# The last group of experts: the overflow loop between its two pairs, the second pair's weights loaded ahead of it, rows returned by index in halves, own sum first

## The chip, the cores and the metric

The kernel runs on one core of a Trainium2 chip. The metric is the device time of one execution in microseconds (us). TensorE is PE in the rows, VectorE DVE, ScalarE ACT, GpSimd POOL and SyncE SP; SP issues most of the DMA transfers, POOL those that go by an index.

## The reference, cut to what matters

512 tokens of 1024 features go through two blocks of a transformer. The first ends with a hierarchical mixture of experts: each token picks one of 4 groups and, in it, 2 of 8 experts with hidden width 256. The second begins with a norm and a sparse attention layer (DSA) and goes on with more layers. All tensors are fp32. What the change touches is the end of the first block and the start of the second:

```
for g in range(N_GROUPS):                       # 4 groups of 8 experts
    a = einsum('td,edf->tef', t, w_gate[sl]);  u = einsum('td,edf->tef', t, w_up[sl])
    hid = silu(a) * u * combine[:, g, :, None]  # combine: 0 but for a token's 2 experts
    y = y + einsum('tef,efd->td', hid, w_down[sl])
x = x + gt2[:, None, :] * ffn
...
return rms_norm(x, g_final)                     # end of block 1
h = rmsnorm(x, g_attn[0]); proj = h @ w_in      # start of block 2 (DSA)
```

## The kernel before, in words

The activations lie transposed in `xT`: eight blocks `k` of 128 features x 512 tokens. `moe` runs the 32 experts in eight units of four; a unit is two pairs, and each expert takes 64 slots. A ninth unit (`None` in `units`) takes tokens that found no slot. For a pair `q` of unit `u`, written (u,q) here, `up` multiplies the gathered tokens with the gate and up weights of both experts (32 matmuls, `s<-wm,xg`) and makes `hid` on ACT and DVE; `down` transposes `hid` (`o`), copies it (`ht`) and multiplies with the down weights (16 matmuls, `t<-wm,ht`). `load_expert` brings an expert in as four gate/up tiles and two down tiles of 512 KB each, issued by SP; all have the tag `wm`, of which there are 12 buffers, so the 12 tiles of one pair fill the tag and a tile's load waits until the tile 12 places before it has been read.

Units 0 to 6 and the ninth write their result rows by an index to a table in DRAM (`ydr`, issued by POOL). Unit 7 keeps its rows on the core as a rounded part and a rest (`yh`, `yl`); `scatter` adds them to `xT` by matmul with a 0/1 matrix `dt` (`mm<-dt,yh`, `mm<-dt,yl`, four for each `k`), and DVE adds the result to `xT[:, k]`. `combine` fetches the table's rows back, two per token: eight gathers of 128 rows x 1024 by index on POOL (`yg<-ydr,yrowi`), weighted on ACT and added on DVE. `add_combined` transposes that sum on PE (`mm<-ident,yg`, 32 of them) and adds it to `xT` on DVE.

Before the change the order in `moe` is: (7,0) up and down, `combine`, (7,1) up and down, `add_combined`, the overflow loop, `scatter`. The overflow loop (`For_i(0, n)`) handles overflow beyond the ninth unit; with these inputs `n` is 0 and its body is not run. All engines go through its branches all the same. `norm_dsa` loads two weights of the DSA layer (`a_w_idx`, `a_w_in`) into `wm` buffers, and ACT and POOL split them (`wf`); it is called when unit 7 starts, so these loads stand on SP's queue ahead of unit 7's weights.

`scatter(prev, range(KD), done)` calls `done(k)` once `xT[:, k]` is complete: it makes the norm's squares (`sq`: two on ACT, their sums on DVE and on POOL) and the split of the normed block (`xh` on ACT, `xl` on DVE), and PE multiplies these with `wf` (48 matmuls `s<-xh,wf`, `s<-xl,wf`). After the last block PE sums the squares (`o<-ones,sq`) and goes on with the projections of DSA (`mm<-xh,wh` and the like), whose weights arrive as `wr` and are split into `wh` (ACT) and `wl` (DVE or POOL). The masks `ms` and `cm` of DSA are made on POOL in the same stretch. Instructions of one engine run in the order of their queue, which the tile scheduler fixes when the kernel is built.

Of the kernel before, what the change touches and what calls it, by code (L numbers as in the profile page):

```python
# [9 lines left out]
F32 = mybir.dt.float32  # L10
# [8 lines left out]
KD = 8  # L19
# [16 lines left out]
class Kern:  # L36
# [804 lines left out]
    def route(self, rn, pl):  # L841
# [173 lines left out]
        st.yrow = ph.tile([128, 4, 2], I32, name="yrowi")  # L1015
        nc.vector.tensor_copy(st.yrow, yrow)
# [30 lines left out]
    def down(self, st, q, ws, hid):  # L1047
# [28 lines left out]
        if yh:  # L1076
            st.ys.append((yh, yl))

# [94 lines left out]
    def combine(self):  # L1173

        nc, r = self.nc, self.rt
        zs = []
        for t in range(4):
            y = []
            for j in range(2):
                w = self.ph.tile([128, 2, 512], F32, tag="wm", name="yg", bufs=12).rearrange("p h n -> p (h n)")  # L1180
                nc.gpsimd.indirect_dma_start(out=w, out_offset=None, in_=self.ydr[:, :],
                                             in_offset=bass.IndirectOffsetOnAxis(ap=r.yrow[:, t, j:j + 1], axis=0))
                y.append(w)
            nc.scalar.activation(out=y[0], in_=y[0], func=AF.Copy, scale=r.wts[:, t, 0:1])
            nc.vector.scalar_tensor_tensor(out=y[1], in0=y[1], scalar=r.wts[:, t, 1:2], in1=y[0], op0=OP.mult, op1=OP.add)
            zs.append(y[1])
        return zs

    def add_combined(self, zs):
        nc = self.nc  # L1190
        for k in range(KD):
            pt = self.bank("mm")
            for t in range(4):
                nc.tensor.transpose(pt[:, 128 * t:128 * t + 128], zs[t][:, 128 * k:128 * k + 128], self.ident)
            nc.vector.scalar_tensor_tensor(out=self.xT[:, k], in0=pt, scalar=self.mod[:, 40 + k:41 + k], in1=self.xT[:, k], op0=OP.mult, op1=OP.add)

    def moe(self, done=None):
# [23 lines left out]
        for j, u in enumerate(units):  # L1221
            m = len(st.es)
            if st.row is None:
                self.untranspose(st)
            nxt = None
            if j + 1 < len(units):
                u = units[j + 1]
                nxt = self.over_unit(r.oslot, r.ids, Y_OVER) if u is None else self.base_unit(u)
            for q in range(m):
                x = self.up(st, q, lambda e: self.early.pop(e) if isinstance(e, int) and e in self.early else self.load_expert(e))  # L1230
                if nxt is not None:
                    self.gather(nxt, range(4 // m * q, 4 // m * (q + 1)))
                self.down(st, q, *x)
                if nxt is None and q == 0:
                    zs = self.combine()
            prev, st = st, nxt
            if done and j == len(units) - 2:
                self.norm_dsa()
        self.add_combined(zs)
# [4 lines left out]
        nc.vector.tensor_copy(ids2, r.ids[:, 0:16])  # L1244
        with self.tc.For_i(0, n, 1):
            nc.vector.tensor_scalar(os2, os2, -128.0, None, op0=OP.add)
            t = ph.tile([1, 16], I32, name="idst")
            nc.vector.tensor_copy(t[:, 0:14], ids2[:, 2:16])
            nc.vector.tensor_copy(ids2[:, 0:14], t[:, 0:14])
            st = self.over_unit(os2, ids2)  # L1250
            self.gather(st, range(4))
            self.untranspose(st)
            self.down(st, 0, *self.up(st, 0, self.load_expert))
            self.scatter(st, range(KD))
        self.scatter(prev, range(KD), done)
# [743 lines left out]
```

## Time and profile before

| | us |
|---|---|
| median of 3 runs | 1982.56 |
| lowest and highest run | 1979.72, 1983.92 |
| profiled execution | 1980.94 |
| its span in the trace | 1979.2 |
| its mean granted TensorE clock | 0.981 of full speed |
| PE busy, of the span | 1894.1 (96%) |
| DVE, ACT, POOL busy | 951.0 (48%), 743.9 (38%), 292.5 (15%) |

The trace is of one execution, the profiled one; its times count from the start of the span. The change touches some 120 us of it, from about 690 to 810. PE's 96% is busy time of pipelined matmuls, and it averages stages with different limits: where weights stream in at full rate, DMA sets the pace, and PE is merely seldom idle for long. So the stretch is read by what each engine waits for in it.

### The profile page before, as it was taken

What the parts mean: (1) busy time and instruction counts of PE and PEld (TensorE: products, weight loads), DVE (VectorE), ACT (ScalarE), POOL (GpSimd) and SP (SyncE); (2) the same over time, 40 slices, a digit from 0 to 9 for tenths busy, and PEclk for the clock granted to TensorE, in tenths of its full rate; (3) what the DMA queues carried; (4) which work ended last, traced back from release to release, by engine and by line L of the source; (5) the groups of instructions that cost most, each with busy time, mean ns of one, the idle gap of its engine ahead of it and who ended that gap; (6) DMA issues with size and microseconds to landing.
All of it is one profiled execution on the core that took longest, in us unless ns stands there. A gap on an engine that the chain in (4) does not pass through costs nothing.

```text
span 1979.2 us, 26110 instructions
## 1 busy us (share of the span) xinstructions
PE 1894.1 (96%) x9778; PEld 1453.0 (73%) x9778; DVE 951.0 (48%) x2024; ACT 743.9 (38%) x1374; POOL 292.5 (15%) x353
## 2 busy tenths in 40 slices
PE   9999999999988868889999999999999999999998
PEld 6777778885544325568888888887889988888886
DVE  5677764461000025766644444464366553444343
ACT  3555552232211224556332322341455444223233
POOL 2212220000011024575000000000143300000001
PEclk9999999999999988879999999999999999999999
DMA  7523648347999994011223222225410122323221
GB/s 263 189 95 124 206 146 271 111 162 296 365 367 359 358 353 160 33 33 43 96 93 99 96 96 96 96 97 180 139 44 23 43 97 85 96 96 96 96 97 63
DMA packets 91328, 289.85 MB, mean 146 GB/s; under 512 B 13694, under 2 KB 14718, under 8 KB 91200
## 3 DMA queue, kind: packets, MB, share of 16 engines
q1 hardware_dynamic: 87520, 280.35, 40.5%
q0 software_dynamic: 3392, 7.29, 1.0%
q8 instruction: 78, 1.28, 0.3%
q10 hardware_dynamic: 288, 0.52, 0.1%
q14 instruction: 50, 0.41, 0.1%
HBM read 274.02 MB, written 18.35 MB: 148 GB/s over the span
## 4 chain that ended last, share of the span: by engine, by line
PE 55%; DVE 2%; POOL 1%; issue 1%; ACT 1%; DVEq 0%; POOLq 0%; ACTq 0%
PE mm L50 38%; PE s L50 7%; PE t L50 5%; PE o L50 4%; PE t L245 1%; DVE sc L1438 1%; POOL qal L65 0%; DVE m L1437 0%; DVE p L231 0%; POOL p L236 0%; POOL wl L65 0%; POOL ql L65 0%; PE t L1595 0%; DVE sc L1420 0%; POOL sc L1423 0%
## 5 line engine op out<-in xcount | busy, mean ns | idle before, releaser
L61 ACT CAST wh<-wr 128x1024 fp32r<-128x1024 f32 (+1 forms) x222 | 230.9, 1041 | 577.6 <-PE mm L50 312.6
L67 DVE TENSOR_TENSOR wl<-wr,wh 128x1024 fp32r<-128x1024 f32 (+1 forms) x216 | 263.9, 1222 | 315.2 <-ACT wh L61 311.9
L50 PE MATMUL mm<-xh,wh 128*128 128x512 f32 (+1 forms) x640 | 252.6, 395 | 0.0
L50 PE MATMUL mm<-xl,wh 128*128 128x512 f32 (+1 forms) x640 | 250.1, 391 | 0.0
L50 PE MATMUL mm<-xh,wl 128*128 128x512 f32 (+1 forms) x640 | 250.0, 391 | 0.0
L50 PE MATMUL s<-wm,xg 128*64 128x512 f32 x528 | 139.2, 603 | 5.6 <-DMA wm<-in_w_gu 5.4
L50 PEld LDWEIGHTS mm<-xh,wh 128*128 128x128 f32 (+1 forms) x640 | 119.9, 187 | 28.4 <-issue 2.2
L50 PEld LDWEIGHTS mm<-xh,wl 128*128 128x128 f32 (+1 forms) x640 | 119.9, 187 | 26.0
L50 PEld LDWEIGHTS mm<-xl,wh 128*128 128x128 f32 (+1 forms) x640 | 119.8, 187 | 25.0 <-issue 0.5
L234 ACT ACTIVATE p<-p,mx 128x128 f32<-128x128 f32 (+3 forms) x160 | 89.7, 561 | 91.9 <-DVE mx L233 87.4
L50 PEld LDWEIGHTS s<-wm,xg 128*64 128x64 f32 x528 | 42.0, 138 | 85.9 <-issue 73.5
L1044 DVE TENSOR_TENSOR hid<-hid,s 128x256 f32<-128x256 f32 x17 | 7.2, 421 | 199.5 <-ACT hid L1043 199.5
L50 PE MATMUL mm<-hidh,wh 128*128 128x512 f32 x256 | 99.6, 389 | 0.0
L50 PE MATMUL mm<-hidl,wh 128*128 128x512 f32 x256 | 99.6, 389 | 0.0
L50 PE MATMUL mm<-hidh,wl 128*128 128x512 f32 x256 | 99.6, 389 | 0.0
L236 POOL TENSOR_SCALAR p<-p,mx 128x128 f32<-128x128 f32 (+3 forms) x96 | 60.1, 629 | 153.0 <-DVE mx L235 97.5
L50 PE MATMUL mm<-hh,wh 128*128 128x512 f32 x192 | 77.9, 407 | 1.5 <-ACT hh L61 1.5
L231 DVE CUSTOM_DVE_ANT_0 p<-s,ms 128x256 f32<-128x256 f32 (+3 forms) x128 | 61.3, 487 | 35.6 <-PE s L50 30.2
L50 PE MATMUL mm<-hl,wh 128*128 128x512 f32 x192 | 76.4, 398 | 0.8 <-DVE hl L67 0.8
L50 PE MATMUL mm<-hh,wl 128*128 128x512 f32 x192 | 75.9, 395 | 0.0
L245 PE MATMUL t<-ident,p 128*128 128x128 f32 x400 | 69.8, 281 | 6.0 <-POOL p L236 5.8
L61 ACT CAST hidh<-r 128x512 fp32r<-128x512 f32 x64 | 39.7, 621 | 85.0 <-DVE r L1259 85.0
(607 smaller groups left out, 3984.3 us busy)
## 6 DMA issues: line engine op xcount, KB each, us to landing
wm<-in_w_gu SPq DMA_DIRECT2D x132, 512.0 KB
wm<-in_w_dn SPq DMA_DIRECT2D x66, 512.0 KB
wr<-in_w_up SPq DMA_DIRECT2D x64, 512.0 KB
wr<-in_w_down SPq DMA_DIRECT2D x64, 512.0 KB
wr<-in_w_ada SPq DMA_DIRECT2D x48, 512.0 KB
wr<-in_w_in SPq DMA_DIRECT2D x22, 512.0 KB
ydr<-zero SPq DMA_DIRECT2D x32, 256.0 KB
wr<-in_cmp_w SPq DMA_DIRECT2D x16, 512.0 KB
```

Of the source, the lines that this page charges most:

```text
L50: return self.nc.tensor.matmul(ps, lhsT=l, rhs=r, start=start, stop=stop)
L61: nc.scalar.copy(hi, src)
L67: return nc.vector.tensor_tensor(out=lo, in0=src, in1=fv(hi), op=OP.subtract)
L231: nc.vector.tensor_tensor_reduce(out=p[:, :n], in0=s[:, :n], in1=master[:, c0:c0 + n], scale=1.0, scalar=-3.0e38, op0=OP.add, op1=OP.max, ...
L234: nc.scalar.activation(out=p[:, :n], in_=p[:, :n], func=AF.Exp, bias=mx[:, 1:2], accum_out=mx[:, 2:3])
L236: nc.gpsimd.tensor_scalar(p[:, :n], p[:, :n], mx[:, 3:4], 1.0 if gate is None else gate, op0=OP.mult, op1=OP.mult)
L245: nc.tensor.transpose(ps[:, b], p[:, b], self.ident)
L1044: nc.vector.tensor_tensor(out=hid, in0=hid, in1=ps[:, 256:512], op=OP.mult)
L1438: nc.vector.match_replace(out=sc[:, :n], in_to_replace=m8, in_values=sc[:, :n], imm_value=-3.0e38)
```

## The change

1. In `moe` the order becomes: (7,0) up and down; both experts of (7,1) loaded; the overflow loop; (7,1) up and down; `combine`; `norm_dsa`; `scatter`; `add_combined`. The ninth unit and units 1 to 6 are as before.
2. `combine` fetches rows in halves of 512 columns: 16 gathers of 128 x 512 instead of 8 of 128 x 1024, from the same table seen as rows twice as many, with two index tiles (`yrowi0`, `yrowi1`). They go into buffers of another pool and no longer into `wm`. A copy of one column of a weight tile of (7,1) on POOL (`mark`) stands ahead of the gathers.
3. The unit's own rows are added first (`scatter`, without `done`), the fetched ones last, and `add_combined` calls `done(k)`.
4. The body of the loop uses narrow buffers of its own (`narrow_pair`); `no_sync_barrier` is called ahead of the loop.
5. `norm_dsa` moves behind the loop, and with it the loads of `a_w_idx`, `a_w_in` and of nine small vectors (gains of norms).

The core of the diff:

```diff
-        st.yrow = ph.tile([128, 4, 2], I32, name="yrowi")
-        nc.vector.tensor_copy(st.yrow, yrow)
+        st.yrow = [ph.tile([128, 4, 2], I32, name=f"yrowi{h}") for h in range(2)]
+        for h in range(2):
+            nc.vector.tensor_scalar(st.yrow[h], yrow, 2.0, float(h), op0=OP.mult, op1=OP.add)
...
-    def combine(self):
+    def combine(self, behind):
         nc, r = self.nc, self.rt
+        ydr = self.ydr.rearrange("n (f d) -> (n f) d", f=2)
+        mark = self.small.tile([128, 1], F32, tag="mark", name="mark", bufs=1)
+        last = nc.gpsimd.tensor_copy(mark, behind)
         zs = []
-        for t in range(4):
-            y = []
-            for j in range(2):
-                w = self.ph.tile([128, 2, 512], F32, tag="wm", name="yg", bufs=12).rearrange("p h n -> p (h n)")
-                nc.gpsimd.indirect_dma_start(out=w, out_offset=None, in_=self.ydr[:, :],
-                                             in_offset=bass.IndirectOffsetOnAxis(ap=r.yrow[:, t, j:j + 1], axis=0))
-                y.append(w)
...
+        for h in range(2):
+            z = []
+            for t in range(4):
+                y = []
+                for j in range(2):
+                    y.append(self.X("yg"))
+                    with self.tc.issue_after(last.ins):
+                        nc.gpsimd.indirect_dma_start(out=y[j], out_offset=None, in_=ydr,
+                                                     in_offset=bass.IndirectOffsetOnAxis(ap=r.yrow[h][:, t, j:j + 1], axis=0))
+                nc.scalar.activation(out=y[0], in_=y[0], func=AF.Copy, scale=r.wts[:, t, 0:1])
+                nc.vector.scalar_tensor_tensor(out=y[1], in0=y[1], scalar=r.wts[:, t, 1:2], in1=y[0], op0=OP.mult, op1=OP.add)
...
+        self.down(st, 0, *self.up(st, 0, load))
+        ws = [self.load_expert(e) for e in st.es[1]]
+        behind = ws[1][0][0][:, 0:1]
         n = nc.values_load(r.ids[0:1, 16:17], min_val=0, max_val=7)
...
+        self.tc.no_sync_barrier()
         with self.tc.For_i(0, n, 1):
...
-        self.scatter(prev, range(KD), done)
+        self.down(st, 1, *self.up(st, 1, lambda e: ws.pop(0)))
+        zs = self.combine(behind)
+        if done:
+            self.norm_dsa()
+        self.scatter(st, range(KD))
+        self.add_combined(zs, done)
```

**The queue of SP around the loop.** Before: the two DSA weights, then four experts' weights (unit 7), then the loop's branches; the last row is that in front of which the engine goes on behind a loop that is not run.

```order
L1285 DMA wm<-in_a_w_idx 128x576
L1285 DMA wm<-in_a_w_in 128x1024
L1025 DMA wm<-in_w_gu 128x1024 x4
L1029 DMA wm<-in_w_dn 128x1024 x2
L1025 DMA wm<-in_w_gu 128x1024 x4
L1029 DMA wm<-in_w_dn 128x1024 x2
L1025 DMA wm<-in_w_gu 128x1024 x4
L1029 DMA wm<-in_w_dn 128x1024 x2
L1025 DMA wm<-in_w_gu 128x1024 x4
L1029 DMA wm<-in_w_dn 128x1024 x2
L1245 COMPARE_AND_BRANCH
```

After: the same unit's last two weight tiles, the loop's branches with what SP waits for on the way past the body, and what follows the loop. Semaphores `DMAHW0` to `DMAHW7` count the transfers that SP issues.

```order
L1031 DMA wm_6225<-in_w_dn 128x1024 [waits DMAHW6_49,PE_49]
L1031 DMA wm_6227<-in_w_dn 128x1024 [waits DMAHW7_49,PE_49]
L1293 COMPARE_AND_BRANCH
L1293 UNCONDITIONAL_BRANCH [waits SP_sequencer_49,DMAHW0_49,DMAHW1_49,DMAHW2_49,DMAHW3_49,DMAHW4_49,DMAHW5_49,DMAHW6_49,DMAHW7_49]
...
L352 DMA v_g_mlp1_13828<-in_g_mlp1 128x8 [waits DMAHW4_49]
L1338 DMA wm_6601<-in_a_w_idx 128x576 [waits DMAHW5_49,PE_49]
L1338 DMA wm_6612<-in_a_w_in 128x1024 [waits DMAHW6_49,PE_49,Pool_49]
...
L1317 DMA ms_7524<-in_rel_bias_2 128x512 [waits DMAHW6_49,PE_49]
L87 DMA wr_6866<-in_a_w_in 128x1024 [waits DMASW4_49,DMASW3_49,DMASW5_49,DMASW2_49,DMASW6_49,DMASW1_49,DMASW7_49,DMASW0_49,DMAHW7_49,DVE_49,Pool_49]
```

The DSA weights moved from ahead of unit 7's weights to behind the loop. The way past the loop's body carries a wait on all eight counters of SP's transfers; in the program the values waited for are those of every transfer issued up to there (752 on each counter in the kernel after, 768 or 784 in the one before), and the other engines wait for the same counters before they go on. The first projection weight `wr` now waits for all gathers (`DMASW`), for DVE and for POOL; in the kernel before it has no wait.

**The queue of POOL behind the last table write.** Before (`wf`: split of the DSA weights; `yg`: the gathers):

```order
L1066 DMA ydr<-y,wrow 4352x512
L65 TENSOR_TENSOR wf<-wm,wf 128x512 x2
L1181 DMA yg<-ydr,yrowi 128x1024 x8
L1240 TENSOR_LOAD ids
L1245 COMPARE_AND_BRANCH
L1245 UNCONDITIONAL_BRANCH x2
```

After, from the loop's end to the first split of a projection weight:

```order
L1219 COPY mark<-wm 128x1
L1228 DMA yg<-ydr,yrowi_4406 128x512 x8
L1228 DMA yg<-ydr,yrowi_4407 128x512 x8
L1318 AFFINE_SELECT ms<-ms 128x512 x2
L65 TENSOR_TENSOR wf<-wm,wf 128x288
...
L65 TENSOR_TENSOR wf<-wm,wf 128x512
L1318 AFFINE_SELECT ms<-ms 128x512
L1442 MEMSET cm 128x512
L1443 AFFINE_SELECT cm<-cm 128x512
L179 TENSOR_TENSOR sq<-sq 128x512 x5
L65 TENSOR_TENSOR wl<-wr,wh 128x1024 x3
```

The gathers and the four `wf` moved behind the loop and stand ahead of the squares; the first `wl` moved from between the second and the third `sq` to behind the last.

**The queue of DVE behind the loop.** Before, from unit 7's last `yl` on, it holds 8 additions to `xT` (L1121), 8 `xl` and 7 `sq` up to the sums. After, it begins so:

```order
L1046 TENSOR_TENSOR hid<-hid,s 128x256
L68 SCALAR_TENSOR_TENSOR yl<-t,cws,yh 128x512
L1161 SCALAR_TENSOR_TENSOR xT<-mm,mod,xT 128x512
L68 SCALAR_TENSOR_TENSOR yl<-t,cws,yh 128x512
L1161 SCALAR_TENSOR_TENSOR xT<-mm,mod,xT 128x512 x4
L1231 SCALAR_TENSOR_TENSOR yg<-yg,wts 128x512
L1161 SCALAR_TENSOR_TENSOR xT<-mm,mod,xT 128x512
L1231 SCALAR_TENSOR_TENSOR yg<-yg,wts 128x512
```

It goes on with six more `yg`, eight additions of fetched rows (L1242), 7 `sq` and 8 `xl`: from the first `yl` to the last `xl` 41 instructions of 512 columns. Eight `yg` of 512 (four of 1024 before), eight additions and the `yl` moved behind the loop.

## Rows read from the trace of the kernel before

**Rows 1.** Page, part 2: GB/s moved in each of 40 slices.

```profile
GB/s 263 189 95 124 206 146 271 111 162 296 365 367 359 358 353 160 33 33 43 96 93 99 96 96 96 96 97 180 139 44 23 43 97 85 96 96 96 96 97 63
```

**Rows 2.** Windows: stretch, length, busy time of each engine, PEclk, DMA share, GB/s.

```profile
708.00:712.00 4.00, 2.24 (x6) 0.68 (x8) 0.00 (x0) 0.00 (x0) 1.23 (x2) 0.75 1.02 410
...
748.00:756.00 8.00, 4.69 (x20) 1.26 (x18) 1.92 (x3) 2.13 (x4) 0.00 (x0) 1.00 0.02 6
```

**Rows 3.** Timeline of PE: start, length, instruction, count, [idle before, releaser].

```profile
709.76 8.78 PE L50 MATMUL s<-wm,xg 128*64 128x512 f32 x30 [4.03 <-DMA wm<-in_w_gu]
722.33 0.44 PE L1051 MATMUL o<-ident,hid 128*128 128x128 f32 x2 [3.79 <-DVE hid L1044]
723.28 5.35 PE L50 MATMUL t<-wm,ht 128*64 128x512 f32 x16 [0.52 <-issue]
...
741.52 7.08 PE L50 MATMUL s<-wm,xg 128*64 128x512 f32 x30
...
750.43 3.65 PE L50 MATMUL t<-wm,ht 128*64 128x512 f32 x16 [0.46 <-ACT ht L1053]
757.16 0.50 PE L50 MATMUL mm<-dt,yh 128*128 128x512 f32 x1 [3.07 <-DVEq L1245]
```

**Rows 4.** Timeline of SP's queue of DMA issues, same columns.

```profile
691.45 0.33 SPq L1285 DMA_DIRECT2D wm<-in_a_w_idx  x1
...
742.19 0.85 SPq L1029 DMA_DIRECT2D wm<-in_w_dn  x2
```

**Rows 5.** Timeline of DVE, same columns.

```profile
741.07 1.41 DVE L1195 SCALAR_TENSOR_TENSOR xT<-mm,mod,xT 128x512 f32<-128x512 f32 x2 [0.19 <-PE mm L1194]
...
753.23 0.75 DVE L68 SCALAR_TENSOR_TENSOR yl<-t,cws,yh 128x512 fp32r<-128x512 f32 x1 [3.75 <-ACT yh L63]
754.88 0.75 DVE L68 SCALAR_TENSOR_TENSOR yl<-t,cws,yh 128x512 fp32r<-128x512 f32 x1 [0.91 <-ACT yh L63]
...
782.67 1.78 DVE L179 TENSOR_TENSOR sq<-sq 128x512 f32<-128x512 f32 x1
```

**Rows 6.** Groups on DVE, 757 to 787: shapes, count, busy us, mean ns, idle before.

```profile
L179 DVE TENSOR_TENSOR sq<-sq 128x512 f32<-128x512 f32 x7 | 8.5, 1212 | 0.0
L68 DVE SCALAR_TENSOR_TENSOR xl<-xT,v_g_attn,xh 128x512 fp32r<-128x512 f32 x8 | 8.1, 1006 | 0.1
L1121 DVE SCALAR_TENSOR_TENSOR xT<-mm,mod,xT 128x512 f32<-128x512 f32 x8 | 5.9, 745 | 5.3 <-PE mm L50 5.3
```

**Rows 7.** Groups on POOL, 757 to 787, same columns.

```profile
L179 POOL TENSOR_TENSOR sq<-sq 128x512 f32<-128x512 f32 x7 | 10.5, 1502 | 7.6 <-ACT sq L176 7.6
L1265 POOL TENSOR_SCALAR_AFFINE_SELECT ms<-ms 128x512 f32<-128x512 f32 x8 | 8.0, 1018 | 0.0
L65 POOL TENSOR_TENSOR wl<-wr,wh 128x1024 fp32r<-128x1024 f32 x1 | 2.4, 2412 | 0.0
```

**Rows 8.** Timeline of POOL, columns as in rows 3.

```profile
704.63 1.55 POOL L65 TENSOR_TENSOR wf<-wm,wf 128x288 fp32r<-128x288 f32 x2 [0.79 <-ACT wf L61]
...
711.76 2.51 POOL L65 TENSOR_TENSOR wf<-wm,wf 128x512 fp32r<-128x512 f32 x2
...
724.77 0.94 POOL L1181 DMA_INDIRECT yg<-ydr,yrowi  x1 [0.31 <-issue]
...
757.32 0.61 POOL L1390 TENSOR_SCALAR_AFFINE_SELECT cm<-cm 128x512 f32<-128x512 f32 x1
...
784.89 1.26 POOL L179 TENSOR_TENSOR sq<-sq 128x512 f32<-128x512 f32 x1
```

**Rows 9.** Tile yg: its gathers' time from issue to landing.

```profile
DMA to landing us min/median/max: 7.5/7.8/8.7
```

**Rows 10.** Timeline of PE at the end of the stretch, columns as in rows 3.

```profile
786.20 1.05 PE L50 MATMUL o<-ones,sq 128*128 128x1 f32 x8 [0.65 <-POOL sq L179]
787.12 0.49 PE L50 MATMUL mm<-xl,wh 128*128 128x512 f32 x1
...
793.17 0.40 PE L50 MATMUL mm<-xh,wl 128*128 128x512 f32 x1
```

More of the change, by code (lines that the diff above doesn't have):

```diff
@@ L1077, in down, with narrow_pair, load @@
             st.ys.append((yh, yl))
+    def narrow_pair(self, st):
+        nc, ph = self.nc, self.ph
+        def load(i, src):
+            w = ph.tile([128, 2, 512], F32, tag=("d", "dc")[i % 2], name="wn", bufs=1)
+            nc.sync.dma_start(w, src)
+            return w
+        ps = self.bank("s")
+        for e in range(2):
+            s = bass.ds(st.es[0][e], 1)
+            for c in range(4):
+                w = load(c, self.A["w_gu"][s, c].rearrange("a p k n -> p (a k) n"))
+                for k in range(2):
+                    self.mm(ps[64 * e:64 * e + 64], st.xg[2 * c + k][:, 64 * e:64 * e + 64], w[:, k], c == 0 and k == 0, c == 3 and k == 1)
+        hid = ph.tile([128, 256], F32, tag="hid", name="hid", bufs=2)
+        nc.scalar.activation(out=hid, in_=ps[:, 0:256], func=AF.Silu)
+        nc.vector.tensor_tensor(out=hid, in0=hid, in1=ps[:, 256:512], op=OP.mult)
+        pt = self.bank("o", (128, 2, 128))
+        for f in range(2):
+            nc.tensor.transpose(pt[:, f], hid[:, 128 * f:128 * f + 128], self.ident)
+        ht = ph.tile([128, 2, 128], F32, tag="ht", name="ht", bufs=2)
+        nc.scalar.copy(ht, pt)
+        py = [self.bank("t") for _ in range(2)]
+        for e in range(2):
+            s = bass.ds(st.es[0][e], 1)
+            for f in range(2):
+                w = load(f, self.A["w_dn"][s, f].rearrange("a p (h n) -> p (a h) n", h=2))
+                for half in range(2):
+                    self.mm(py[half][64 * e:64 * e + 64], ht[:, f, 64 * e:64 * e + 64], w[:, half], f == 0, f == 1)
+        yh, yl = [], []
+        for half in range(2):
+            h, l = [(self.O, self.X)[half](n, F32R) for n in ("yh", "yl")]
+            self.split(py[half], h, l, st.ws[0])
+            yh.append(h)
+            yl.append(l)
+        st.ys.append((yh, yl))
     def gather(self, st, parts, late=False):
@@ L1193, in add_combined @@
             for t in range(4):
[L1194 removed]
+                nc.tensor.transpose(pt[:, 128 * t:128 * t + 128], zs[k // 4][t][:, 128 * (k % 4):128 * (k % 4) + 128], self.ident)
             nc.vector.scalar_tensor_tensor(out=self.xT[:, k], in0=pt, scalar=self.mod[:, 40 + k:41 + k], in1=self.xT[:, k], op0=OP.mult, op1=OP.add)
+            if done:
+                done(k)
     def moe(self, done=None):
@@ L1220, in moe @@
         units = [0, None] + list(range(1, 8))
-        for j, u in enumerate(units):
+        load = lambda e: self.early.pop(e) if isinstance(e, int) and e in self.early else self.load_expert(e)
+        for j, u in enumerate(units[1:] + [7]):
             m = len(st.es)
```

36 lines of the change are left out of this document (14 added, 22 removed).

## The prediction

> **What bounds the kernel now.** I read the slices of the span first: from the tenth to the fifteenth they move about 360 GB/s [rows 1]; these are the experts, so weights set the pace there. At the change's place the windows say the same in detail, 410 GB/s with the DMA engines fully busy in 708 to 712, and then a stretch with nothing to move, 748 to 756 at a share of 0.02 [rows 2]: the last weights have landed and the experts' tail follows. Next PE's timeline, which has four things to see [rows 3]. Pair (7,0) begins at 709.76 after 4.03 us of waiting for weights. Its `down` is late: `o` waits 3.79 us for `hid`, and the 16 `t` end at 728.63, 10.1 us after `up` (709.76 + 8.78 = 718.54). Pair (7,1) has `up` from 741.52 to 748.60 and the end of `t` at 754.08, 5.5 us after `up`; I use that as the undisturbed length. And PE waits 3.07 us at the overflow loop, restarting at 757.16, 1.5 us after DVE's last `yl` (754.88 + 0.75) [rows 5]. Behind the loop the limit is another one: PE, DVE and POOL go round the eight blocks of `xT`, and the stretch ends when DVE's last `sq` is done (784.45), POOL's last (786.15) and PE's sums (787.25) [rows 5, 8, 10]. From 787.12 on PE runs the projections back to back [rows 10]. So 709.76 to 787.25 is what the change can shorten.
>
> **Part 1, ahead of the loop: earlier weights.** The loads of `a_w_idx` and `a_w_in` (288 and 512 KB by their shapes) no longer stand ahead of unit 7's [rows 4]: 0.82 MB at 410 GB/s [rows 2], 2.0 us. (7,0) starts at 709.76 - 2.0 = 707.8. Its 30 matmuls took 8.78 us where the same 30 of (7,1) took 7.08, behind a clock of 0.75 [rows 2, 3]; I take 8.1 between them, so 715.9. The weighting of fetched rows on ACT, which held `hid`, is gone from here, so `down` takes 5.5 and ends at 721.4 instead of 728.6: 7.2 us earlier.
>
> **Part 2: the wait that the loop adds.** The 12 tiles of (7,1) go into the 12 buffers of (7,0). Eight come free during its `up`, four only as the last matmuls of its `down` read them, about 721. By the program's order nothing passes the loop before the eight counters have reached all of SP's transfers. Before, they had: the last weights were issued at 742.19 and the queue was empty from 748 [rows 2, 4]. Now the branch stands right behind the last issue, and every engine waits for all of (7,1)'s weights. Queued on PE behind it is `up` of (7,1), which needs only the first tiles to begin, and everything after it. Four tiles of 524 KB at 410 GB/s are 5.1 us: data until 727 to 728. Between the last data and the signal I allow 0 to 3 us (no row separates them) and for crossing 1.5 as above: PE restarts between 728.5 and 732.5, and I take 731. That is 9.6 us of idle PE. It will run `up` at the low clock again: 32 matmuls at 7.08/30 are 7.55, and the (7,0) rows show 1.7 more behind a wait; 9.25. With 5.5 for `down`, `t` ends at 731 + 9.25 + 5.5 = 745.8. Against PE's restart behind the loop before, 757.16, that is **11.4 us ahead**, the loop being passed already.
>
> **Part 3: what moves behind it.** Before, the fetched rows were weighted and added while the weights of (7,1) came in, and cost nothing. Now they stand between own rows and the norm. DVE then has 41 instructions of 512 columns from the first `yl` to the last `xl` (2 `yl`, 8 + 8 additions to `xT`, 8 `yg`, 7 `sq`, 8 `xl`), where before it had 23 behind the loop. Two of them in a row take 1.41 us for the first's 0.75, a pitch of 0.665 [rows 5]: 27.3 us. To this comes what POOL does to DVE: beside it `sq` takes 1.21 and `xl` 1.01 on average, 8.5 + 8.1 us where 15 x 0.665 would be 10.0 [rows 6]: 6.6 us. The same 15 run again; POOL has its `wf` more, but is busy with gathers earlier; I keep 6.0. DVE's waits are the unknown: before, 5.3 us, of which 3 at the loop [rows 6]; I take 2.5, for the last fetched rows. Its first `yl` starts 0.85 before the end of `t` [rows 3, 5], at 745.0, so DVE ends at 745.0 + 27.3 + 6.0 + 2.5 = 780.8, 3.6 before its 784.45. The sums end 2.8 us behind DVE's end before (787.25), set by POOL's last `sq` [rows 10]; with the same tail now 783.6: **3.6 us gained of 11.4**; 7.8 are given back.
>
> **The gathers.** POOL issues one in 0.94 us with 0.31 between [rows 8], 1.25, for 128 rows of 4 KB. For rows of 2 KB no row shows it: 0.63 if it goes by bytes, 1.25 if it goes by the number of rows; I take 1.25, since 0.94 of it is the instruction itself, and keep the other for the rival that is faster. 16 take 20 us, from 731.6 to 751.6. They landed 7.5 to 8.7 us after issue [rows 9], beside weights; at 7.8 the last is in at 759.4 and its sum on DVE at about 760.7. DVE is through the 21 instructions queued ahead of it at 745.0 + 14 = 759. So the halves are hidden but for some 2 us, part of the 2.5. A rule bears on this. The Trainium skill ("DMA: Bandwidth & Descriptors", section "Anatomy of one DMA — SWDGE (gpsimd) path") gives a transfer issued by GpSimd about 2.0 us plus its bytes at 436 GB/s; that speaks against halves, since the fixed part is paid twice, but for 256 KB it makes 2.6 us, and an estimate by it lands the last half at 754.2, so that DVE would never wait and the sum would be 2.5 less. The row says 7.8 for 512 KB, three times what the page gives (3.2), though in a busy queue; after the change the queue is nearly empty.
>
> **Part 4, small terms.** Eight projection matmuls ran inside the stretch before (24 of the first weight's, of which 20 stand from 787.12 to 793.57, and four of the second's); now `wr` is loaded later and they follow the sums, at a pitch of 0.23 [rows 10]: +1.8. The nine vector loads and the two DSA weights run when nothing else moves. `mark` waits for a tile that the loop has waited for: nothing. **Sum:** -3.6 + 1.8 = -1.8 on the profiled execution, 1980.94 - 1.8 = 1979.1. That execution lies 1.6 below the median of the runs; brought to the median, 1982.56 - 1.8 = 1980.8.
>
> **The rivals.** *Fetched rows land early and contention falls (faster).* With the queue empty, landing takes less (I assume half of 7.8), or the halves issue faster; then DVE never waits (-2.5), and POOL, busy with gathers until 751.6, disturbs fewer of the `sq` and `xl` (half of 6.0, -3.0): 1980.8 - 5.5 = 1975.3. For it: the empty queue in 748 to 756 [rows 2]. Against: POOL's work isn't less, only later, where the `sq` and `xl` are. By the page's figure of 2.6 us the landing half of it alone gives 1978.3.
>
> *POOL becomes the bound (slower).* Behind the gathers POOL has 8 `ms` (8.0), 7 `sq` (10.5), four `wf` (1.55 + 2.51) and `cm`'s two steps (0.61 for one, as much taken for the other): 23.8 us [rows 7, 8], then the first `wl` (2.4). It can't start `wf` before ACT's part, which stands on ACT's queue behind the weighting of the last rows, about 758. Without a further wait POOL's last `sq` ends at 781.8 and `wl` at 784.2, just as PE wants it for its third projection matmul. It waited 7.6 us for ACT in the old round [rows 7]; if 5 of that recur, the sums end at 781.8 + 5 + 1.1 = 787.9 and `wl` comes at 789.2, and PE's stretch starts some 5.5 later than in my sum: 1986.3. The point from which this decides is 2 us of waits on POOL. It is helped by the `wr` loads, which wait for the last `wf` (about 771) and need some 4 to 5 us to come in.
>
> *The loop does not hold (the change does what it says).* If weights stream through the loop, PE runs `up` as tiles land, ends `t` some 6 us earlier, and DVE, the next limit, gains about as much: 1975 or, with DVE's waits for rows growing, 1977. The program's order speaks against it.
>
> **How the numbers follow.** A measurement of this kernel can tell about 0.2% (4 us) from no change. Forecast, about the same: 0.42. Rows early or less contention: 0.27. POOL as the bound: 0.25. The loop not holding: 0.06. The first rival and the last are counted as faster: 0.33. The range takes in the restart between 728.5 and 732.5 and both first rivals, 1974.5 to 1989; it leaves out deeper tails of both, about 0.2.
>
> **What would show it.** Right: PE idle some 10 us at the loop with DMA busy, restarting at 731 (part 2); `t` of (7,1) done near 746; gathers from 731 at 1.25 each; DVE nearly without gaps from 746 to 781; sums near 784. Wrong: PE's restart before 727 (the loop doesn't hold); landing under 4 us; POOL or `wl` named as the releaser of the sums and the first projections, with PE idle behind 785 (POOL's rival). The forecast falls if the seven `sq` and eight `xl` cost less than 13 or more than 19 us on DVE.

## The result, and the profile after

| kernel | median, us | runs | profiled execution | span | mean clock |
|---|---|---|---|---|---|
| before | 1981.14 (1979.67 to 1983.92) | 4 | 1980.94 | 1979.2 | 0.981 |
| after | 1998.59 (1996.56 to 2003.02) | 4 | 1996.59 | 1994.8 | 0.975 |

The ratio is 1.0089, with a 95% interval of 1.0066 to 1.0113. The change makes the kernel slower by about 17 us. The forecast was 1980.8, about the same, with a range that ended at 1989: it was wrong, and the range did not hold the time.

The timeline of PE in the kernel after (start, length, instruction, count, idle before and its releaser) answers to [rows 3]:

```profile
706.96 7.08 PE L50 MATMUL s<-wm,xg 128*64 128x512 f32 x30 [0.94 <-DMA wm<-in_w_gu]
...
715.93 3.65 PE L50 MATMUL t<-wm,ht 128*64 128x512 f32 x16 [0.52 <-ACT ht L1055]
...
730.46 9.79 PE L50 MATMUL s<-wm,xg 128*64 128x512 f32 x32 [10.88 <-SPq L1293]
...
744.04 0.44 PE L1053 MATMUL o<-ident,hid 128*128 128x128 f32 x2 [2.66 <-issue]
...
747.84 6.21 PE L50 MATMUL t<-wm,ht 128*64 128x512 f32 x16 [3.36 <-issue]
...
799.67 2.36 PE L50 MATMUL o<-ones,sq 128*128 128x1 f32 x16
```

Three things are to be seen. Pair (7,0) is early and runs without a gap: `t` ends at 719.58 (728.63 before). The loop then holds PE for 10.88 us, released by SP's queue at the loop's line, L1293. And `t` of (7,1) ends only at 754.05, 13.8 us after the end of `up` (730.46 + 9.79 = 740.25), where the same step took 5.5 before. It ended at 754.08 before, so all that the earlier weights gave is lost by here. The sums end at 802.03, 14.8 later than in [rows 10].

SP's queue, same columns, to be set beside [rows 4]:

```profile
719.64 0.86 SPq L1031 DMA_DIRECT2D wm<-in_w_dn  x2
731.43 0.34 SPq L352 DMA_DIRECT2D v_g_final<-in_g_final  x1
...
781.61 0.80 SPq L87 DMA_DIRECT2D wr<-in_a_w_in  x2
```

The last weights are issued 22.6 us earlier than before (742.19), and then SP stands at the loop until 731. The first load of `wr` stands behind POOL's last `wf` and is issued at 781.61.

The windows (stretch, length, busy time of PE, its weight loads, DVE, ACT and POOL, PEclk, DMA share, GB/s) answer to [rows 2]:

```profile
724.00:732.00 8.00, 1.54 (x4) 0.54 (x6) 0.00 (x0) 0.00 (x0) 1.07 (x2) 0.50 0.50 198
...
740.00:744.00 4.00, 1.38 (x6) 0.67 (x4) 0.42 (x1) 0.38 (x1) 3.09 (x4) 1.00 1.02 364
744.00:748.00 4.00, 0.60 (x4) 0.36 (x6) 0.00 (x0) 0.37 (x1) 3.09 (x4) 0.77 1.01 390
748.00:752.00 4.00, 4.00 (x10) 1.08 (x12) 0.00 (x0) 0.00 (x0) 3.37 (x5) 0.50 0.89 288
```

From 740 to 748 PE, DVE and ACT do little; POOL issues gathers, and the DMA engines are full. From 748 to 752 PE works on `t` without a break, at a granted clock of 0.50.

ACT's timeline shows who kept PE waiting:

```profile
743.15 0.38 ACT L1045 ACTIVATE hid<-s 128x256 f32<-128x256 f32 x1 [22.81 <-DMA ms<-in_rel_bias]
747.41 0.37 ACT L1055 COPY ht<-o 128x256 f32<-128x256 f32 x1 [3.88 <-issue]
753.77 1.26 ACT L63 ACTIVATE yh<-t,cws 128x512 fp32r<-128x512 f32 x2 [5.98 <-remote]
...
766.69 0.63 ACT L176 ACTIVATE sq<-xT 128x512 f32<-128x512 f32 x1 [8.59 <-DVE xT L1242]
...
769.58 0.41 ACT L61 CAST wf<-wm 128x288 fp32r<-128x288 f32 x1
```

`hid` waits for `s` alone, which ended at 740.25, and starts at 743.15. `ht` waits for `o`, which ended at 744.48, and starts at 747.41. The first `yh` waits for the first half of `t`, modelled to end at 751.52, and starts at 753.77. The releasers in the brackets (a DMA, "issue", "remote") are not what these instructions wait for, which says that the releasing event does not lie at the modelled end of the matmul. The trace's records of PE's semaphore say the same: PE's signal is recorded 2.87 us behind the matmul's end for `hid` and 2.23 for `yh`, and in the rest of this stretch, as in the kernel before, 0.01 to 0.14. For `o` there is no record; many are missing. PE's ends are modelled, so whether the matmul ended late or its signal was held can't be told; "late signal" below stands for either. ACT's and DVE's own signals are not late here: ACT's `hid` ends at 743.53 and DVE's starts at 743.57, which ends at 743.99, and PE's `o` starts at 744.04.

POOL's timeline, beside [rows 8]:

```profile
730.40 0.18 POOL L1219 COPY mark<-wm 128x1 f32<-128x1 f32 x1 [18.30 <-SPq L1293]
731.12 1.01 POOL L1228 DMA_INDIRECT yg<-ydr,yrowi  x1 [0.53 <-issue]
...
749.95 0.95 POOL L1228 DMA_INDIRECT yg<-ydr,yrowi  x1 [0.30 <-issue]
...
770.08 1.14 POOL L65 TENSOR_TENSOR wf<-wm,wf 128x288 fp32r<-128x288 f32 x1 [18.00 <-ACT wf L61]
...
795.05 2.80 POOL L65 TENSOR_TENSOR wl<-wr,wh 128x1024 fp32r<-128x1024 f32 x1
```

Sixteen gathers at a pitch of 1.25, then 18 us of waiting for ACT's `wf`, then work to the end. DVE's groups from 754 to 799 and one of POOL's, beside [rows 6, 7]:

```profile
L68 DVE SCALAR_TENSOR_TENSOR xl<-xT,v_g_attn,xh 128x512 fp32r<-128x512 f32 x8 | 10.7, 1341 | 5.5 <-ACT xh L63 5.5
L179 DVE TENSOR_TENSOR sq<-sq 128x512 f32<-128x512 f32 x7 | 7.9, 1132 | 0.1
...
L179 POOL TENSOR_TENSOR sq<-sq 128x512 f32<-128x512 f32 x7 | 9.8, 1403 | 4.9 <-ACT sq L176 4.9
```

### The profile page after: what moved, and what is told of

Same layout as the page of the kernel before. It is cut to its first block, busy times and chain, and to the rows that moved or that the text cites. A ratio compares the mean times of both kernels' runs of the same rounds, so it can differ in the third digit from the quotient of the medians.

```text
span 1994.8 us, 26136 instructions
## 1 busy us (share of the span) xinstructions
PE 1897.6 (95%) x9778; PEld 1453.2 (73%) x9778; DVE 952.4 (48%) x2029; ACT 743.5 (37%) x1378; POOL 295.5 (15%) x362
## 4 chain that ended last, share of the span: by engine, by line
PE 55%; POOL 3%; DVE 2%; issue 2%; ACT 1%; DVEq 0%; POOLq 0%; ACTq 0%
PE mm L50 37%; PE s L50 8%; PE t L50 5%; PE o L50 4%; PE t L245 1%; POOL yg L1228 1%; DVE sc L1491 1%; POOL qal L65 0%; DVE m L1490 0%; DVE sc L1473 0%; DVE p L231 0%; POOL wl L65 0%; POOL ms L1318 0%; POOL ql L65 0%; ACT sq L176 0%
## 5 line engine op out<-in xcount | busy, mean ns | idle before, releaser
L50 PE MATMUL t<-wm,ht 128*64 128x512 f32 x264 | 64.6, 620 | 9.1 <-ACT ht L1055 5.7
```

What stands on the lines that cost most here:

```text
L50: return self.nc.tensor.matmul(ps, lhsT=l, rhs=r, start=start, stop=stop)
```

## Experiments

After the result I had three suspects: the loop's hold on all engines; `wf`, which had moved into the round of squares on ACT and POOL; and PE's late signals beside the gathers. Every run is compared with the kernel before on the same chip; the ratio is what counts.

**1. The DSA weights back ahead of unit 7.**

```diff
+        if done:
+            self.norm_dsa()
         self.down(st, 0, *self.up(st, 0, load))
...
         zs = self.combine(behind)
-        if done:
-            self.norm_dsa()
```

> The changed kernel with one part undone: norm_dsa is called where the kernel before calls it, so the two DSA weights load ahead of unit 7's weights and their four splits (wf) stand ahead of the gathers on POOL and ahead of the added rows on ACT. Theory 'wf queue' (in the changed kernel POOL stands idle from 752 to 770 because wf on ACT is queued behind a square that waits for DVE's first fetched row block, and POOL then works without a break to 798): POOL's squares start with DVE's, its last ends about 10 us earlier than in the changed kernel relative to the end of pair (7,1)'s t, total about 1988 to 1990. Rival 'DVE': the 41 instructions of DVE set the end whatever POOL does; then the sums move by less than 3 us and the total stays at 1994 or above. Under both, the two stalls of ACT between PE's last s and the yh of (7,1) (3 us each, 8 in sum) stay.

Measured: 1990.37, ratio 1.0037 (1.0023 to 1.0052). PE restarts at 736.08, 5.6 later than in the kernel after, since 0.8 MB is back in front, and the time still falls, by the ratios by about 10 us: `wf` is done before unit 7, and POOL's idle stretch of 17.3 us ends in squares alone. `hid` is on time here and `ht` 1.1 late; the second `yh` starts 7.2 us behind the end of `t` (759.22 for 751.99).

**2. Without the loop** (which runs no iteration on these inputs; the overflow's part of the computation is left out).

```diff
-        n = nc.values_load(r.ids[0:1, 16:17], min_val=0, max_val=7)
...
-        with self.tc.For_i(0, n, 1):
...
-            self.scatter(so, range(KD))
```

> The changed kernel with the overflow loop left out (with these inputs its body is never run). Theory 'hold': PE's 10.9 us in front of pair (7,1) shrink to the time in which tiles arrive; up of (7,1) ends when its last tiles have landed, about 730 instead of 740, and if ACT's three late starts come from the branch (code fetched anew behind it) they go as well: t ends about 735 instead of 754, total 1980 to 1984. If ACT's late starts come from the DMA traffic or the gathers, they stay: t ends about 742, total 1987 to 1990. If neither hold nor late starts matter because POOL's tail is paced by its own gathers and splits, the total falls by less than 4 us.

Measured: 1988.21, ratio 1.0023 (1.0011 to 1.0036). `up` of (7,1) starts at 724.67 and `t` ends at 737.2, 17 us before the kernel after; PE's timeline has only a 2.18 wait for weights:

```profile
724.67 7.08 PE L50 MATMUL s<-wm,xg 128*64 128x512 f32 x30 [2.18 <-DMA wm<-in_w_gu]
```

But the sums begin at 790.53, only 9 us earlier: the additions to `xT` then wait for PE's signals, recorded 2 to 3.4 us late, and POOL waits 14.5 us for `wf`. So the hold is real: without the loop the time is lower by 10 to 13 us (by medians and by ratios), and the rest is not the loop's.

**3. Both together**, the edits of experiments 1 and 2 (again without the loop).

> Both undone at once: norm_dsa ahead of unit 7 as in the kernel before, and the overflow loop left out (its body is never run with these inputs). The changed kernel took 1998.6, with norm_dsa early 1990.4, without the loop 1988.2. If the two costs lie one behind the other on the path (the hold 10 us, the wf queue 8 us), they add: 1980 to 1981. If the late PE signals beside the gathers (each 2 to 3 us) are what takes over, part of the gain goes: 1983 to 1986. Nothing in it should be below 1978 while PE's signals stay late.

Measured: 1982.92, ratio 1.0000 (0.9987 to 1.0013). All of the change's loss is gone, but the two costs do not add in full: by the ratios the single steps gave 10 and 13 us, and both together 17.6, between what was expected if they add and if the late signals take over. `t` ends at 744.0, and then PE stands idle for 9.40 us in front of an addition, while its signals are recorded 5 to 9 us late; the last gather is issued at 750.74.

**4. The gathers behind the last `yl`.**

```diff
-        zs = self.combine(behind)
+        zs = self.combine(st.ys[1][1][1][:, 0:1])
```

> The changed kernel with one thing moved: the mark in front of the 16 gathers copies from the last yl of (7,1) instead of from a weight tile, so the gathers are issued only when (7,1) is done; the loads of DSA weights and masks stay where they are. Theory 'gathers delay ACT': hid, ht and yh of (7,1) start within 0.5 us of PE's results, t ends near 746 instead of 754. Rival 'SP's loads or the branch delay ACT': the three late starts stay, t ends at 752 to 754. Either way the last fetched row lands about 28 us after t's end instead of at about 754, so the total is longer than the changed kernel's, 2005 to 2015.

Measured: 2000.3, ratio 1.0079 (1.0062 to 1.0096). `hid`, `ht` and both `yh` follow PE at once (ACT's `hid` at 743.87 names its releaser, PE `s`), though SP's loads keep the DMA engines at 0.96 there. The gain is lost again: the gathers run from 751.8 to 772.9, and the sums begin at 805.60. The late rows are only part of that, as one instruction of DVE shows:

```profile
770.05 0.75 DVE L1231 SCALAR_TENSOR_TENSOR yg<-yg,wts 128x512 f32<-128x512 f32 x1 [0.78 <-DMA yg<-ydr,yrowi]
...
772.77 11.07 DVE L1231 SCALAR_TENSOR_TENSOR yg<-yg,wts 128x512 f32<-128x512 f32 x1 [1.37 <-DMA yg<-ydr,yrowi]
```

The same weighting of a row, 0.75 us elsewhere, takes 11.07, and in just this time POOL, through with its gathers, runs its masks, `wf` and squares back to back (772.88 to 783.29). These 10.3 us on DVE are not the rows' late landing. The same is seen in experiments 10 (4.22 us, beside POOL's masks and a square) and 13 (3.97, beside masks). That POOL's work holds DVE is likely from these three; no run moved POOL's work away.

**5. Only the gathers beside PE's work.** As experiment 1, and POOL's loads of `ms` held back until the last `yl`, so that nothing but gathers moves.

```diff
+        self.nc.vector.tensor_copy(m[:, 0:1], self.late)
         self.nc.sync.dma_start(m, self.A["rel_bias_2"][h])
```

> The changed kernel with norm_dsa early, and the loads of the masks (ms, 8 x 256 KB) held until the last yl of (7,1), by a tiny DVE copy into each mask tile ahead of its load. So nothing but the 16 gathers moves while (7,1) computes. Theory 'gathers and SP's transfers together': PE's signals come within 0.1 us of its ends, t of (7,1) ends about 751 (restart 736 + 15), total 1983 to 1986 if the later masks don't cost. Theory 'gathers alone': the yh still start 2 us or more after PE's ends, t's signals come as late as with norm_dsa early alone (yh at 754 and 759 for t's halves at 750 and 752), total 1988 to 1992.

Measured: 1993.75, ratio 1.0057 (1.004 to 1.0074). A window and ACT's timeline:

```profile
752.00:756.00 4.00, 2.11 (x10) 0.80 (x6) 0.75 (x1) 0.69 (x1) 2.87 (x4) 1.00 0.72 210
```

```profile
753.88 0.69 ACT L63 ACTIVATE yh<-t,cws 128x512 fp32r<-128x512 f32 x1 [4.58 <-PE t L50]
760.96 0.69 ACT L63 ACTIVATE yh<-t,cws 128x512 fp32r<-128x512 f32 x1 [6.39 <-remote]
```

The DMA engines are far from full (0.72, 210 GB/s), PE has ended `t` at 753.01, and the second `yh` still starts at 760.96, 2.8 us after the last gather's issue ended (758.17). Full DMA engines are not what delays the signals. Four of PE's signals are recorded here within 0.12 us of each other, 760.93 to 761.05, though PE's last matmul before them ended at 756.36; the last record of the last gather's landing lies at 760.93. In experiment 1 it is the same: 759.20 to 759.31, the matmul's end at 757.45, the landing at 759.16.

**6. The gathers in two groups of eight.** As experiment 1, the second eight behind the last `yl`.

```diff
+            if h:
+                mark = self.small.tile([128, 1], F32, tag="mark2", name="mark2", bufs=1)
+                last = nc.gpsimd.tensor_copy(mark, behind2)
```

> The changed kernel with norm_dsa early and the second eight gathers held behind the last yl of (7,1); the first eight stay at the loop's end. Theory 'many gathers in a row': in the kernel before and in the one with own buffers PE's signals were on time beside eight gathers, and the late ones came from the eighth or ninth on; so here signals are on time for (7,1), t ends about 751, the second eight land about 751 + 10 + 3 = 764, beside DVE's other work, total 1984 to 1988. Rival 'any gather beside a full queue': late signals stay and the second eight come later still, total 1991 to 1995.

Measured: 1985.0, ratio 1.0009 (0.9995 to 1.0023): one signal late by 1.35, the others on time, and 5.5 us less than experiment 1.

**7. The same split alone**, the edit of experiment 6 in the kernel after.

> The kernel after with one edit: the second eight gathers wait for the last yl of pair (7,1); the DSA weights stay behind the loop. Theory (long rows of gathers on POOL delay PE's signals, and that costs on its own): PE restarts at 730.5 as in the kernel after, ACT's hid follows the end of s at 740 within 0.5 us, t ends near 747 instead of 754, second gathers 749 to 759; the queue of wf on ACT and POOL stays as it is but begins some 6 us earlier, sums end near 796, time near 1992. Rival (the loss at PE's signals is covered by the wait of POOL for wf, which ends when the fetched rows are added): t ends early but the squares on ACT still wait for the fetched rows, the sums end at 800 to 803 and the time stays at 1997 to 2000.

Measured: 1992.06, ratio 1.0041 (1.0027 to 1.0055). The theory's 1992 is met in part by luck, on a chip whose kernel before took 3 us more, and not by its path: `hid` is still 3.03 late (PE's `s` ends at 741.63, its signal is recorded at 744.66, 1.6 us after the eighth gather), `t` runs at the low clock (5.35 us), and it ends at 751.83; after that every signal is on time. So eight in a row do not rule the delay out, they shorten it.

**8. The loop ahead of unit 7** (with experiment 1's order).

```diff
+        w0 = [self.load_expert(e) for e in st.es[0]]
         n = nc.values_load(r.ids[0:1, 16:17], min_val=0, max_val=7)
...
+        self.down(st, 0, *self.up(st, 0, lambda e: w0.pop(0)))
+        ws = [self.load_expert(e) for e in st.es[1]]
```

> The changed kernel with norm_dsa early and the overflow loop moved ahead of unit 7, with the weights of (7,0) issued in front of it. The loop then holds every engine until (7,0)'s weights have landed (about 713 instead of 708 for the first use), and (7,1)'s weights stream behind it without a hold. Theory: the hold costs 5 us there instead of 15 (norm_dsa early: restart at 736), t of (7,1) ends about 742 to 745, total 1983 to 1986. Rival: SP can issue nothing behind the loop until (7,0) has landed, so the queue runs empty there as well and the weights of (7,1) come 5 to 8 us later than without the loop; with the late signals beside the gathers the total stays at 1988 to 1992.

Measured: 1990.93, ratio 1.0036 (1.0023 to 1.0049). PE waits 14.55 us in front of (7,0) instead. By the ratios the hold costs as much there as in front of (7,1) in experiment 1: it moves with the loop, as weights are in flight at both places.

**9. The order of before, with only the gathers as sixteen halves in buffers of their own.**

```diff
-                w = self.ph.tile([128, 2, 512], F32, tag="wm", name="yg", bufs=12).rearrange("p h n -> p (h n)")
...
+                    y.append(self.X("yg"))
+                    nc.gpsimd.indirect_dma_start(out=y[j], out_offset=None, in_=ydr,
```

> The kernel before with one part of the change: rows return in 16 halves into buffers of their own instead of 8 whole rows into the weight buffers; the order (gathers behind (7,0), loop behind both pairs) is as before. In the kernel before, (7,1)'s weights wait for buffers that hold fetched rows (SP waits 13.3 us for DVE's yg and 6.4 for PE's transposes). Theory: that wait goes, the weights of (7,1) stream on and land about 728 to 730 instead of 748, t of (7,1) ends near 740 instead of 754, total 1968 to 1972. Rival: the 16 gathers take 20 us on POOL and their traffic shares the DMA engines with the weights, and ACT's weighting of rows stands ahead of hid, so PE's (7,1) starts late all the same; gain under 5 us, 1977 to 1981.

Measured: 1987.26, ratio 1.0019 (1.0008 to 1.003). SP no longer waits for buffers that hold fetched rows, and the last weights are issued by 727.2 instead of 743.0. Little of that arrives: PE waits 6.85 us for weights and starts `s` of (7,1) at 732.23, ACT weights a fetched row (742.49) in front of `hid` (743.12), and `t` ends at 751.73, 2.4 us earlier than before. POOL and SP are past the loop at 757.6, but PE's first matmul behind it is late:

```profile
761.93 0.80 PE L50 MATMUL mm<-dt,yh 128*128 128x512 f32 x1 [6.13 <-DMA wr<-in_a_w_in]
```

It does not use `wr`. In this stretch the trace records instruction fetches at 757.7, 758.5 and 763.3, among the loads of `wr`; that the fetch is what PE waits for is likely, and not shown.

**10. `wf` ahead of the rows.**

```diff
+        if done:
+            self.norm_dsa()
         zs = self.combine(behind)
-        if done:
-            self.norm_dsa()
```

> The kernel after with one edit: norm_dsa is written ahead of combine, so POOL's four wf and four ms stand ahead of the gathers, ACT's part of wf ahead of the weighting of rows; the loop holds as before and the DSA weights are still loaded behind it. Theory (the wait of POOL for wf on ACT, 18 us, is what makes POOL the bound): wf is done by 750, gathers run 750 to 770 and land by 773, PE's signals for hid and ht are on time, DVE then has four blocks of xT, sq and xl behind the last rows, sums near 789, time near 1986. Rival (the fetched rows are what all waits for, whichever queue holds them): sums near 800, as in the kernel with late gathers, time 1996 to 2000.

Measured: 1991.41, ratio 1.004 (1.0026 to 1.0055), between the two. `t` ends at 746.77, no signal is late, `wf` is done at 753.7. But the gathers run from 753.87 to 775.6, and PE then goes at their pace (2.5 us for a pair of them):

```profile
765.14 0.69 PE L1241 MATMUL mm<-ident,yg 128*128 128x128 f32 x2 [2.10 <-DVE yg L1231]
```

**11. Rows by plain loads.** Sixteen loads of the same size from fixed rows, on SP's queue, in place of the gathers; the rows that are added are therefore not the wanted ones.

```diff
-                        nc.gpsimd.indirect_dma_start(out=y[j], out_offset=None, in_=ydr,
-                                                     in_offset=bass.IndirectOffsetOnAxis(ap=r.yrow[h][:, t, j:j + 1], axis=0))
+                        i = 1024 * h + 256 * t + 128 * j
+                        nc.sync.dma_start(y[j], ydr[i:i + 128, :])
```

> The kernel after with one edit: the sixteen gathers by index are replaced by sixteen plain loads of 128 x 512 from fixed rows of the table, issued by SP at the same place, so the rows that are added are not the wanted ones (this part of the computation is changed). Theory (the gathers themselves delay PE's signals): hid follows the end of s at 740 within 0.5 us, ht and yh likewise, t of (7,1) ends at 746 to 747 instead of 754, and the time falls by 5 to 8 us, to 1991 to 1994; wf on POOL still waits for ACT, which stands behind squares. Rival (any transfers of this size behind the loop delay them): hid 2 us late or more, t ends at 752 or later, time 1996 or more.

Measured: 1982.4, ratio 0.9996 (0.998 to 1.0012), 9 us lower than the theory asked. Timelines of PE, ACT and POOL, and a window:

```profile
729.57 8.69 PE L50 MATMUL s<-wm,xg 128*64 128x512 f32 x32 [11.79 <-SPq L1293]
...
740.10 3.65 PE L50 MATMUL t<-wm,ht 128*64 128x512 f32 x16 [0.46 <-ACT ht L1055]
...
785.58 1.84 PE L50 MATMUL o<-ones,sq 128*128 128x1 f32 x16
```

```profile
738.31 0.38 ACT L1045 ACTIVATE hid<-s 128x256 f32<-128x256 f32 x1 [19.77 <-PE s L50]
```

```profile
758.53 1.23 POOL L65 TENSOR_TENSOR wf<-wm,wf 128x288 fp32r<-128x288 f32 x1 [15.60 <-ACT wf L61]
...
774.36 2.78 POOL L65 TENSOR_TENSOR wl<-wr,wh 128x1024 fp32r<-128x1024 f32 x1
```

```profile
738.00:742.00 4.00, 3.54 (x18) 1.63 (x18) 0.42 (x1) 0.76 (x2) 0.90 (x2) 1.00 0.99 348
```

The DMA engines are as full as in the kernel after (0.99, 348 GB/s), the bytes and the buffers are the same, and no signal of PE is late by more than 0.14 us. `t` ends at 743.75 instead of 754.05: `down` takes 5.5 us, as the forecast had it. 0.9 of the 10.3 us come from PE's earlier restart and 1.1 from a shorter `s`. They go on to `wf` (758.53 for 770.08) and, with 3 more since DVE waits 2.5 us for ACT's `xh` instead of 5.5, to the sums (787.42 for 802.03). So the gathers by index on POOL, not the transfers as such, delay PE's signals, and here that is nearly all of the 17 us. The edit takes away two things at once, the index and POOL as the issuing engine; which of them matters was not tried.

**12. Early DSA weights, gathers split, no loop:** the edits of experiments 1, 2 and 6 (the overflow's part is left out again).

> The overflow loop is left out (it runs no iteration on these inputs), the DSA weights are loaded ahead of unit 7 and the second eight gathers wait for the last yl. Theory (three separate costs that add up: the loop's hold, the queue of wf, PE's signals late beside sixteen gathers): the step from the loop's hold, 7.5 us between the two kernels with early DSA weights, adds to the kernel with split gathers at 1985.0, so 1977.5, t of (7,1) ends near 741 and the sums near 786. Rival (behind a t that ends early the fetched rows are the bound, so that splitting the gathers only delays them): sums 791 or later, time 1983 or more.

Measured: 1972.73, ratio 0.9947 (0.9931 to 0.9962), 5 us better than the 1977.5 expected from the single steps, and the only order that is faster than before, by half a per cent and without the overflow's part. PE goes from (7,0) into (7,1) without a gap:

```profile
728.31 7.08 PE L50 MATMUL s<-wm,xg 128*64 128x512 f32 x30
...
737.22 3.65 PE L50 MATMUL t<-wm,ht 128*64 128x512 f32 x16 [0.46 <-issue]
```

The eight gathers from 728.5 to 738.3 delay no signal here.

**13. The same with the loop kept, between `up` and `down` of (7,1).**

```diff
+        rows = self.combine(behind)
+        next(rows)
+        x = self.up(st, 1, lambda e: ws.pop(0))
         n = nc.values_load(r.ids[0:1, 16:17], min_val=0, max_val=7)
...
-        self.down(st, 1, *self.up(st, 1, lambda e: ws.pop(0)))
+        self.down(st, 1, *x)
```

> The kernel with split gathers and early DSA weights, with the overflow loop kept, but behind up of pair (7,1) instead of ahead of it; the first eight gathers stand ahead of the loop, the second eight behind the last yl. Theory (the loop costs what is queued in front of it, and here all weights have landed by the time PE has used them): (7,1)'s 30 matmuls follow (7,0)'s at about 728 without a wait, PE waits at the loop only from 736 until the first eight gathers have landed and been crossed, about 741 to 742; t ends near 747, second gathers 749 to 759, sums some 5 us behind those of the kernel without a loop, time 1977 to 1979. Rival (crossing the loop costs 4 to 6 us in itself, as the first instructions behind it waited where the loop stood behind the last yl): t ends at 751 or later, time 1981 to 1984, no gain over the kernel before.

Measured: 1987.63, ratio 1.0014 (1.0001 to 1.0027): the rival. PE's timeline:

```profile
744.50 0.80 PE L50 MATMUL mm<-dt,yh 128*128 128x512 f32 x1 [8.72 <-DVEq L1301]
...
747.04 5.58 PE L50 MATMUL t<-wm,ht 128*64 128x512 f32 x16
```

All weights had landed, and the loop now waits for the eight gathers (the last issued by 739.7), for ACT's weighting of their rows, behind which `hid` stands (742.04), and for DVE's `hid`; then PE runs `t` at the low clock (5.58 for 3.65). `t` ends at 752.6, and the `yg` of 3.97 us named in experiment 4 adds some 3 us behind it. No version with the loop kept that I ran beats the kernel before.

## Why the prediction was wrong

- **Part 1** held. (7,0) starts at 706.96 (forecast 707.8) and its `t` ends at 719.58 (721.4).
- **Part 2, the hold,** held: PE restarts at 730.46 (731) and `up` takes 9.79 (9.25). That it ends at 740.25, just as by the sum, is luck, as the two misses cancel. Experiments 2 and 12 show that it is the loop: without it (7,1) starts 6 us earlier or follows without a gap.
- **Part 2, the step that failed:** "With 5.5 for `down`". It took 13.8. The 5.5 was called undisturbed and taken from a stretch of before in which POOL issued no gathers, and the forecast had itself put the gathers from 731.6 to 751.6, over just this `down`. It priced them for POOL and for their landing, and gave them no effect on PE and ACT. `hid` and `ht` each started 2.9 us behind PE's end, 5.8 together, and 2.56 came with the clock: behind these waits `t` ran 6.21 us for 3.65, most of it at the lower level of 1.2 GHz (the grant of 748 to 752 is 0.50). That is the 8.3 us by which `down` was too long; the first `yh`, 2.23 late, adds 1.3 for DVE. Experiments 4, 5 and 11 show the cause: signals on time when the gathers are elsewhere, late ones with gathers alone, none late with the same bytes as plain loads, where `down` took the 5.5. No row of the kernel before showed it: its eight gathers delayed no signal.
- **Part 3, DVE.** It starts at 754.49 (745.0 forecast), 9.5 late from the step above, and needs 43.9 us to the last `xl` (35.8). The instructions were right (27.3); contention was 8.6 for 6.0 (`xl` and `sq` 10.7 + 7.9 where 15 x 0.665 is 10.0), and waits 7.9 for 2.5, of which 5.5 are for ACT's `xh`.
- **The gathers.** The pitch of 1.25 was right: a gather of 128 rows takes as long with 2 KB as with 4 KB. Landing was mis-sized in part. The trace has only some of the landing's records; the last one found comes 3.1 us behind the issue of the first and of the last gather, but 5.4 to 6.7 us behind that of those in the middle, where the DMA engines are full. The forecast had 7.8 for all of them from [rows 9], with weights in the queue. The estimate of 2.6 us worked out from the Trainium skill ("DMA: Bandwidth & Descriptors", "Anatomy of one DMA — SWDGE (gpsimd) path") is near only at the two ends. (An estimate by the same page of the Trainium skill for 512 KB is 3.2 us, and 7.8 is 2.4 times that, not three times.) It did not help, as the last record lies at 753.06, before DVE came to the rows.
- **POOL's rival** occurred as a mechanism, and at its own price: POOL waited 4.9 us for ACT's squares (5 assumed). In experiment 11, where the late signals are gone, POOL still waits 15.6 us for `wf` and 3.4 for squares, and the sums end at 787.42 (787.9 in the rival); of its price little reaches the time, 1982.4 (1986.3), as the first `wl` is done before the sums there. In the kernel after it starts 12 us later than the 758 assumed, and of these 9.5 are the late DVE. The other 2.5 are squares that stand on ACT ahead of the first `wf` and wait 8.59 us for the first fetched block.
- **Part 4.** The first projections follow the sums as forecast, but at a pitch of 0.34 (24 in 8.24 us) for 0.23. 0.23 is the pitch at the high clock, and 0.43 that at the low one: the mean grant from 799 to 810 is 0.69. It was misread already: in the kernel before the 20 from 787.12 to 793.57 had taken 0.32 each. The error is small, as the low clock was in the time before too.
- **The loop does not hold** fell, as its chance of 0.06 said.

The sums end 18.4 us later than forecast (802.03 for 783.6): 8.3 from `down`, 1.3 from the first `yh`, 8.1 from DVE's longer stretch, and 0.8 behind it. Without the gathers' effect on PE the time came out near the forecast, the kernel with plain loads being at 0.9996, but in part by luck: its sums end at 787.42, 3.8 later than forecast and where POOL's rival had them, and its projections then run at the pitch of 0.23 behind a `wl` that is done. What was missing is one effect of 8 to 10 us at the head of a chain on which every later step waits, and some 4 us that the later steps added to it: 802.03 - 787.42 = 14.6 at the sums, 16.2 in the time.

Open remains how gathers delay PE's signals. In this stretch of all runs, signals more than 1 us late were recorded only while gathers ran or in the 3.8 us behind the start of the last one's issue, and mostly from the eighth gather in a row on: up to 1.35 and 3.03 late beside eight (experiments 6 and 7; at most 0.3 in 12 and 13), up to 9.3 beside sixteen (experiment 3). But a long row alone does not do it: in experiments 4 and 10, where ACT and DVE took the rows as they landed, the few signals of PE recorded beside the second eight were on time. What the difference is was not tried, nor whether gathers by index issued by another engine, or plain loads issued by POOL, do the same.

## What to carry to other kernels

A loop that usually runs no iteration made every engine wait here for the transfers issued ahead of it, so it belongs where nothing is in flight and nothing is queued in front of it that waits. Rows fetched by index should not run in long groups beside a chain of short steps between PE, ACT and DVE: in the one run that tried it, the same bytes by plain loads, from fixed rows and on SP's queue, delayed nothing there. Gathers by index are not free either where they are moved to: POOL's work that piled up behind them ran beside an instruction of DVE that took 11 us for 0.75 (experiment 4). And a duration taken from an undisturbed stretch holds only if the forecast's own timeline puts nothing new beside it.

## What the hardware showed that was not expected

- PE's semaphore signals were recorded up to 9.3 us behind the modelled end of the matmul beside sixteen gathers by index (experiment 3), 0.01 to 0.14 nearly everywhere away from gathers. ACT's and DVE's signals in the same stretch were on time.
- One DVE instruction of 0.75 us took 11.07, 4.22 and 3.97 while POOL worked back to back beside it (experiments 4, 10 and 13).
- A gather of 128 rows takes POOL 0.95 + 0.30 us whether the rows have 4 KB [rows 8] or 2 KB.
- Behind a loop that was passed at 757.6, PE's first matmul came at 761.93 while loads were in flight (experiment 9).
